# Moving four weight buffers by 64 to 384 bytes in on-chip memory

## The chip, the cores and the metric

The kernel runs on one core of a Trainium2 chip. The metric is the device time of one execution in microseconds (us), taken as the median of several runs. The profile comes from one further execution, recorded by the hardware profiler. The engines are named as in the profile: PE multiplies matrices, PEld is PE's loading of the stationary operand, DVE, ACT and POOL work elementwise, and SP issues most DMA transfers. A partition is one of the 128 rows of the on-chip memory; a "byte offset" below is always an offset within a partition, and "remainder" means the remainder of such an address divided by 2048.

## The reference, cut to what matters

One layer of a sequence model over 512 positions of width 1024, everything in float32. The large products are these:

```python
def _token_mixer(h, ...):
    p = h @ w_in                                    # 1024 -> 3 gates, pooling, latents, u and v
    ...
    y_a = _pool_mixer(a, w_pool, s_pool) @ w_branch[0]
    y_b = _mla(cq, ckv, kr, ...) @ w_branch[1]      # attention, 8 heads
    y_c = _sgu(uv, g_sg, b_sg, w_s, b_s) @ w_branch[2]
    merged = gates[:, :, 0] * y_a + gates[:, :, 1] * y_b + gates[:, :, 2] * y_c
    return merged @ w_o

def _conv_ffn(h, w_up, conv_w, conv_b, w_down):
    z = h @ w_up                                    # 1024 -> 2 * 2816
    ...                                             # causal convolution of width 3
    return (jax.nn.silu(gate) * val) @ w_down       # 2816 -> 1024

def reference(x, c, pos, ...):
    mod = silu(c) @ w_ada[l] + b_ada[l]             # six rows of 1024
    h = _modulate(x, sh_t, sc_t)
    y = _token_mixer(h, ...)
    x = _layer_norm(ALPHA * x + gt_t * y) * ln_t_g[l] + ln_t_b[l]
    h = _modulate(x, sh_f, sc_f)
    y = _conv_ffn(h, ...)
    x = _layer_norm(ALPHA * x + gt_f * y) * ln_f_g[l] + ln_f_b[l]
```

The positions' angles (`_rope_tables`) go through a reduction to one period before sine and cosine; two small tiles of the kernel, `ang` and `kq`, hold them.

## The kernel before

Every float32 operand is split into a high part and a low part in the type float32r: `hi = round(x)`, `lo = x - hi`. A product is then three matrix multiplications, high times low, low times high and high times high, added up in one PSUM tile.

The activations stay on chip. They lie in tiles of 128 partitions by 512 floats (2048 bytes a partition), with 48 buffers in the pool tag `act`, 16 in `h`, 8 in `m` and 8 in `pt`, all in the pool `sb`. The weights stream in. One chunk of weights is 128 by 1024 floats (512 KB): SP's queue loads it into one of three buffers `raw`, ACT casts it to the high part (`whi`, two buffers, line 91), and DVE subtracts to get the low part (`wlo`, two buffers, line 92). The function `wsplit` does this; `prepare`, `scaled_chunk` and `early_split` do the same for the first projection, for the two output projections (there POOL first scales the chunk) and for two chunks at the start of the second half. Both tags have two buffers that take turns, so one chunk is split while PE works on the one before.

PE uses a chunk 24 times, mostly in one of two forms. In `mm_chunk` (lines 112, 113 and 115) the stationary operand is a slice of 128 columns of the chunk and the moving operand is an activation tile of 512 columns: 16 multiplications with the high part (each slice twice, with the low and the high activations), then 8 with the low part. In `uv_half` (lines 846, 848, 849) and in the first loop of `project_out` (lines 1043, 1045, 1046) the stationary operand is a slice of an activation tile and the moving operand is half a chunk: 16 with the high part, then 8 with the low part. For each multiplication PE has a load of its own stationary operand, and the load for the next one runs while the present one streams its moving columns.

A few multiplications read other tiles. The padded tiles (`pad_t`, 528 floats) hold the softmax numerators `pe`, the gated products `uz` and the split rows `adah` and `adal`. `ptp` (line 661) transposes `pe`, `ptz` (line 954) transposes `uz`, and `pgt` (line 744) multiplies `adah` and `adal` by the constant matrix `onesr`.

Where the tiles lie follows from the pools, which are laid out one behind the other: `const`, then `pd` (five padded tiles of 2112 bytes), `sb`, `wp` (the weight buffers) and `sm`. All tiles of `sb` and, before the change, of `wp` are 2048 or 4096 bytes long, so all of them have the same remainder of 2048: 896 in the built program. The padded tile number i (0 to 4) ends up 320 - 64 i bytes short of that remainder, since 2112 is 2048 + 64 and five of them lie ahead of `sb`. `onesr` lies 416 bytes short of it. [...]

The order of the instructions on each engine is set by a scheduler when the kernel is built, within the order of the program text; `issue_after` adds a few constraints.

Of the kernel before, what the change touches and what calls it, by code (L numbers as in the profile page):

```python
# [8 lines left out]
F32 = mybir.dt.float32  # L9
F32R = mybir.dt.float32r  # L10
# [5 lines left out]
P = 128  # L16
S = 512
D = 1024
KT = 8
TT = 4  # L20
# [30 lines left out]
def trunk(ctx: ExitStack, tc: tile.TileContext, A, out):  # L51
    nc = tc.nc

    const = ctx.enter_context(tc.tile_pool(name="const", bufs=1))
    pd = ctx.enter_context(tc.tile_pool(name="pd", bufs=5))
    sb = ctx.enter_context(tc.tile_pool(name="sb", bufs=1))
    wp = ctx.enter_context(tc.tile_pool(name="wp", bufs=2))
# [3 lines left out]
    def ps(name):  # L61
        return pp.tile([P, 512], F32, name=name, tag="ps")
# [4 lines left out]
    def h_t(name, dt=F32R):  # L67
        return sb.tile([P, 512], dt, name=name, tag="h", bufs=16)
# [4 lines left out]
    def pt_t(name, dt=F32):  # L73
        return sb.tile([P, 512], dt, name=name, tag="pt", bufs=8)

    def pad_t(name, dt=F32):
        return pd.tile([P, 528], dt, name=name, tag="pad")

    def f(ap):
        return ap.bitcast(F32)  # L80

    def load(src, n, name):
        raw = wp.tile([P, D], F32, name=name, tag="raw", bufs=3)
        nc.sync.dma_start(out=raw[:, :n], in_=src)
        return raw

    def wsplit(src, n, name):
        raw = load(src, n, name)
        hi = wp.tile([P, D], F32R, name=name + "h", tag="whi")
        lo = wp.tile([P, D], F32R, name=name + "l", tag="wlo")  # L90
        nc.scalar.copy(out=hi[:, :n], in_=raw[:, :n])  # L91
        ins = nc.vector.tensor_tensor(  # L92
            out=lo[:, :n], in0=raw[:, :n], in1=f(hi[:, :n]), op=ALU.subtract
        )
        last_lo[:] = [ins.ins]
        return hi, lo
# [94 lines left out]
    nc.vector.tensor_scalar_add(out=bmod[:, :, 1], in0=cols[:, C_SCT : C_SCT + 8], scalar1=1.0)  # L191


    ang = const.tile([P, TT, 32], F32, name="ang")
    kq = const.tile([P, TT, 32], F32, name="kq")
    cosT, sinT, cosQ, sinQ = (
        const.tile([P, TT, 32], F32, name=name) for name in ("cosT", "sinT", "cosQ", "sinQ")
    )
# [109 lines left out]
    def after_split():  # L308
        order = ExitStack()
        for ins in split_done:  # L310
            order.enter_context(tc.issue_after(ins))
        return order
# [11 lines left out]
    def chunk(key):  # L324
        if key not in plan:
            return wsplit(A[key[0]][key[1:]], D, key[0])
        i = used[0]
        assert plan[i] == key
        for j in (i, i + 1):
            if j < len(plan) and j not in split:  # L330
                split[j] = wsplit(A[plan[j][0]][plan[j][1:]], D, plan[j][0])
        used[0] += 1
        return split[i]
# [55 lines left out]
    def prepare(j):  # L389
        raws = first_raw[j]  # L390
        acc = first_acc[j]
        wh = wp.tile([P, D], F32R, name="w0h", tag="whi")
        wl = wp.tile([P, D], F32R, name="w0l", tag="wlo")
        with after_split():
            for raw, a, b in ((raws[0], 0, NL), (raws[1], NL, NS)):
                nc.scalar.copy(out=wh[:, a:b], in_=raw[:, : b - a])
                nc.gpsimd.tensor_tensor(
                    out=wl[:, a:b], in0=raw[:, : b - a], in1=f(wh[:, a:b]), op=ALU.subtract
                )
        w0s.append((wh, wl))  # L400
        pm = ps("pm")
        for i in range(2):
            for part in range(2):
                nc.tensor.matmul(
                    pm[:, i : i + 1], acc[part][:, i * P : (i + 1) * P], ones[:, 0:1],
                    start=part == 0, stop=part == 1,
                )
        md = sm.tile([P, 2], F32, name="md", tag="md")
        for i in range(2):
            nc.scalar.activation(  # L410
                md[:, i : i + 1], pm[:, i : i + 1], AF.Identity, bias=bmod[:, j, i : i + 1]
            )
        pt = ps("pt")
        for t in range(TT):
            nc.tensor.transpose(
                pt[:, t * P : (t + 1) * P], xs[t][j // 4][:, (j % 4) * P : (j % 4 + 1) * P], ident
            )
        full = pad_t("hfull")
        hh = h_t(f"hT{j}h")
        hl = h_t(f"hT{j}l")  # L420
        nc.scalar.activation(hh, pt, AF.Identity, bias=md[:, 0:1], scale=md[:, 1:2])
        hi = nc.scalar.activation(full[:, :512], pt, AF.Identity, bias=md[:, 0:1], scale=md[:, 1:2])
        lo = nc.gpsimd.tensor_tensor(out=hl, in0=full[:, :512], in1=f(hh), op=ALU.subtract)
        split_done[:] = [hi.ins, lo.ins]
        hT_hi.append(hh)
        hT_lo.append(hl)
# [97 lines left out]

    def rotary_queries():
        wh, wl = wsplit(A["wqr"], D, "wqr")
        for t in range(TT):
            pq = ps("pq")
# [287 lines left out]
    for g in range(4):  # L816
        if g % 2 == 0:
            wh, wl = chunk(("wpool", g // 2))
# [189 lines left out]
    def scaled_chunk(src, gt, name, dst=None):  # L1008
        raw = load(src, D, name)
        for n in range(2):  # L1010
            c = slice(n * 512, (n + 1) * 512)
            nc.gpsimd.tensor_tensor(out=raw[:, c], in0=raw[:, c], in1=gt[n], op=ALU.mult)  # L1012
        if dst is None:
            hi = wp.tile([P, D], F32R, name=name + "h", tag="whi")
            lo = wp.tile([P, D], F32R, name=name + "l", tag="wlo")
            nc.scalar.copy(out=hi, in_=raw)  # L1016
            nc.vector.tensor_tensor(out=lo, in0=raw, in1=f(hi), op=ALU.subtract)  # L1017
            return [hi[:, :512], hi[:, 512:]], [lo[:, :512], lo[:, 512:]]
        his = [dst(f"{name}h{n}") for n in range(2)]
        los = [dst(f"{name}l{n}") for n in range(2)]  # L1020
        for n in range(2):
            c = slice(n * 512, (n + 1) * 512)
            nc.scalar.copy(out=his[n], in_=raw[:, c])
            nc.vector.tensor_tensor(out=los[n], in0=raw[:, c], in1=f(his[n]), op=ALU.subtract)
        return his, los

    def project_out(src, nk, resident, left_hi, left_lo, gt, dst, chain, name):
        acc = [[ps("py" + name) for _ in range(2)] for _ in range(TT)]

        def step(t, n, k, w):  # L1030
            ts_ = slice(t * P, (t + 1) * P)
            mm3(acc[t][n], left_hi[k][:, ts_], left_lo[k][:, ts_], w[0][n], w[1][n], k == 0, k == nk - 1)

        for k in range(nk - resident):
            w = scaled_chunk(src(k), gt, name)
            for rest in range(2):
                for t in range(TT):
                    ts_ = slice(t * P, (t + 1) * P)
                    hh, hl = left_hi[k][:, ts_], left_lo[k][:, ts_]
                    for n in range(2):  # L1040
                        o = acc[t][n]
                        if rest:
                            nc.tensor.matmul(o, hh, w[1][n], start=False, stop=False)  # L1043
                        else:
                            nc.tensor.matmul(o, hh, w[0][n], start=k == 0, stop=False)  # L1045
                            nc.tensor.matmul(o, hl, w[0][n], start=False, stop=False)  # L1046
        ws = {k: scaled_chunk(src(k), gt, f"{name}{k}", dst) for k in range(nk - resident, nk)}
        for t in range(TT):
            for n in range(2):
                for k in range(nk - resident, nk):  # L1050
                    step(t, n, k, ws[k])
            chain(t, acc[t])
# [11 lines left out]
    def early_split(m):  # L1064
        raw = load(A["wup"][m], D, "wup")
        if m in (2, 3):
            wh = wp.tile([P, D], F32R, name="wuph", tag="whi")
            wl = wp.tile([P, D], F32R, name="wupl", tag="wlo")
            uh = [wh[:, :512], wh[:, 512:]]
            ul = [wl[:, :512], wl[:, 512:]]  # L1070
        else:
            alloc = pt_t if m < 2 else act_t
            uh = [alloc(f"uph{m}{n}", F32R) for n in range(2)]
            ul = [alloc(f"upl{m}{n}", F32R) for n in range(2)]
        for n in range(2):
            nc.scalar.copy(out=uh[n], in_=raw[:, n * 512 : (n + 1) * 512])
        early[m] = uh, ul, raw
# [90 lines left out]
    def after_mixer(t, py):  # L1168
        py_o[t] = py
        if t == 0:  # L1170
            early_split(0)
            early_low(0, nc.vector)
            residual_in(0)
            early_split(1)
            early_low(1, nc.gpsimd)
            residual_in(1)
            residual(0, 0)
            residual(0, 1)
            rs_o[0] = ln_finish(st_o[0])
            affine(0)  # L1180
            early_split(2)
            early_low(2, nc.vector)
# [69 lines left out]
    for i in range(NP):  # L1252
        half = []
        for v in range(2):
# [11 lines left out]
            t = pt_t("zc")  # L1266
# [162 lines left out]
```

## Time and profile before

| | |
|---|---|
| median of 2 runs | 991.12 us (990.82 to 991.42) |
| profiled execution | 992.78 us, of which 990.8 us from the first to the last instruction |
| mean granted PE clock | 0.989 of full speed |
| busy: PE, PEld, DVE, ACT, POOL | 956.8, 802.3, 593.8, 392.8, 310.0 us |
| instructions on PE | 4530 multiplications, 4530 loads of a stationary operand |
| read from HBM | 116.30 MB |

A busy time is the time in which the engine had at least one instruction under way. Multiplications overlap in PE's pipeline, so one of them is recorded as longer than the distance to the next. In groups, "389/389/391" are the shortest, the median and the longest duration in nanoseconds, and what follows is when the first and the last of them began.

### The profile page before, as it was taken

The page shows a single profiled execution, that of the slowest core. Times are in us where ns is not written, and L with a number is a line of the kernel's source. Part 1 is how long each engine was busy: PE and PEld are TensorE (multiplying, and loading weights), DVE is VectorE, ACT ScalarE, POOL GpSimd, SP SyncE. Part 2 cuts the span into 40 slices and gives each one's busy share as a digit, 9 for nine tenths or more (in the row PEclk, how much of TensorE's full clock was granted, in tenths as well). Part 3 has the DMA queues.
Part 4 walks back from the last instruction along what each step waited for, and adds up shares of the span by engine and source line. Part 5 has one row for each costly group of instructions (what it writes and reads, how often), then busy time and mean ns, then how long its engine had stood idle before and what let it go on. Part 6 is the DMA issues. An engine that isn't in the chain of part 4 may idle for free.

```text
span 990.8 us, 12225 instructions
## 1 busy us (share of the span) xinstructions
PE 956.8 (97%) x4530; PEld 802.3 (81%) x4530; DVE 593.8 (60%) x923; ACT 392.8 (40%) x656; POOL 310.0 (31%) x311
## 2 busy tenths in 40 slices
PE   4999999999999999999999997999999999999996
PEld 3888888888878888888888876998888888888885
DVE  6947666556686565555433577675655565632367
ACT  3565555543333322422323235554444444422121
POOL 3555111222350022200012756321111121666654
PEclk9999999999999999999999998999999999999999
DMA  9713112135434633373222371133334343343222
GB/s 341 270 36 99 41 59 55 55 101 176 140 126 164 207 118 107 101 246 111 64 96 96 101 249 76 43 112 124 118 116 126 108 136 98 107 127 102 90 85 85
DMA packets 45274, 119.18 MB, mean 120 GB/s; under 512 B 5280, under 2 KB 8736, under 8 KB 45216
## 3 DMA queue, kind: packets, MB, share of 16 engines
q1 hardware_dynamic: 44784, 118.25, 36.5%
q8 instruction: 35, 0.57, 0.2%
q10 hardware_dynamic: 432, 0.17, 0.1%
q14 instruction: 23, 0.19, 0.1%
HBM read 116.30 MB, written 2.10 MB: 119 GB/s over the span
## 4 chain that ended last, share of the span: by engine, by line
PE 82%; DVE 6%; DMA 4%; POOL 3%; issue 2%; ACT 1%; SPq 0%; DVEq 0%; POOLq 0%; ACTq 0%
PE pzu L113 7%; PE pzu L112 7%; PE pzu L115 7%; PE pg L112 4%; PE pg L115 4%; PE pg L113 4%; PE py L112 3%; PE py L113 3%; PE pyd L1045 3%; PE py L115 3%; PE pyd L1043 3%; PE pyd L1046 3%; PE pu L849 3%; PE pu L848 3%; PE pu L846 3%
## 5 line engine op out<-in xcount | busy, mean ns | idle before, releaser
L92 DVE TENSOR_TENSOR wupl<-wup,wuph 128x1024 fp32r<-128x1024 f32 x38 | 47.8, 1258 | 71.8 <-PE pzu L115 45.8
L1012 POOL TENSOR_TENSOR d<-d,gtfb 128x512 f32<-128x512 f32 x44 | 74.3, 1710 | 37.6 <-DMA d<-in_wdn 34.8
L1285 POOL TENSOR_TENSOR zc<-zc 128x512 f32<-128x512 f32 x22 | 29.7, 1349 | 173.7 <-ACT zc L1284 154.1
L379 POOL TENSOR_TENSOR mg<-mg,th 128x512 f32<-128x512 f32 x16 | 31.3, 1958 | 144.1 <-DVE th L376 144.0
L1017 DVE TENSOR_TENSOR dl<-d,dh 128x1024 fp32r<-128x1024 f32 x18 | 29.1, 1614 | 56.2 <-PE pyd L1043 51.0
L91 ACT CAST wuph<-wup 128x1024 fp32r<-128x1024 f32 x38 | 39.9, 1050 | 46.5 <-PE pzu L113 46.5
L92 DVE TENSOR_TENSOR wgl<-wg,wgh 128x1024 fp32r<-128x1024 f32 x22 | 26.9, 1223 | 47.8 <-ACT wgh L91 35.1
L91 ACT CAST wbh<-wb 128x1024 fp32r<-128x1024 f32 x24 | 25.3, 1054 | 69.4 <-PE py L113 50.2
L726 DVE SCALAR_TENSOR_TENSOR ada<-adar,cact,ada 128x512 f32<-128x512 f32 x56 | 49.7, 918 | 0.5 <-DMA adar<-in_ada 0.5
L1016 ACT CAST dh<-d 128x1024 fp32r<-128x1024 f32 x18 | 19.0, 1053 | 62.5 <-PE pyd L1046 37.6
L1267 ACT ACTIVATE zc<-pzu,cols 128x512 f32<-128x512 f32 x44 | 34.2, 779 | 22.1 <-PE pzu L115 17.4
L91 ACT CAST wgh<-wg 128x1024 fp32r<-128x1024 f32 x22 | 23.3, 1059 | 40.1 <-PE pg L113 26.1
L92 DVE TENSOR_TENSOR wsgl<-wsg,wsgh 128x1024 fp32r<-128x1024 f32 x16 | 19.6, 1226 | 32.1 <-ACT wsgh L91 26.2
L92 DVE TENSOR_TENSOR wbl<-wb,wbh 128x1024 fp32r<-128x1024 f32 x24 | 31.0, 1290 | 9.7 <-ACT wbh L91 5.5
L91 ACT CAST wsgh<-wsg 128x1024 fp32r<-128x1024 f32 x16 | 16.8, 1053 | 48.7 <-PE pu L849 44.1
L1270 DVE SCALAR_TENSOR_TENSOR zc<-pzu,cols,zc 128x511 f32<-128x511 f32 x44 | 32.6, 744 | 3.9 <-ACT zc L1267 3.9
L647 POOL TENSOR_SCALAR pe<-pe,mx 128x128 f32<-128x128 f32 (+3 forms) x32 | 17.0, 534 | 54.3 <-DVE mx L646 53.9
L1274 DVE SCALAR_TENSOR_TENSOR zc<-pzu,cols,zc 128x510 f32<-128x510 f32 x44 | 32.6, 745 | 0.8
L1012 POOL TENSOR_TENSOR o<-o,gttb 128x512 f32<-128x512 f32 x16 | 26.7, 1693 | 16.9 <-DMA o<-in_wo 13.8
L1284 ACT ACTIVATE zc<-zc 128x512 f32<-128x512 f32 x22 | 13.9, 631 | 40.5 <-DVE zc L1274 40.4
L779 POOL TENSOR_TENSOR asum<-apad 128x527 f32<-128x527 f32 x8 | 12.2, 1520 | 55.4 <-ACT apad L774 29.3
L376 DVE SCALAR_TENSOR_TENSOR th<-th,py 128x512 f32<-128x512 f32 x16 | 11.0, 686 | 30.9 <-PE py L115 30.9
(1423 smaller groups left out, 3173.9 us busy)
## 6 DMA issues: line engine op xcount, KB each, us to landing
wup<-in_wup SPq DMA_DIRECT2D x44, 512.0 KB, 3.6
adar<-in_ada SPq DMA_DIRECT2D x64, 256.0 KB, 3.8
wb<-in_wb SPq DMA_DIRECT2D x24, 512.0 KB, 3.6
wg<-in_wg SPq DMA_DIRECT2D x22, 512.0 KB, 3.5
d<-in_wdn SPq DMA_DIRECT2D x22, 512.0 KB, 3.5
ada<-in_ada SPq DMA_DIRECT2D x32, 256.0 KB, 5.1
wsg<-in_wsg SPq DMA_DIRECT2D x16, 512.0 KB, 3.5
wa<-in_wa SPq DMA_DIRECT2D x8, 512.0 KB, 3.5
```

Of the source, the lines that this page charges most:

```text
L91: nc.scalar.copy(out=hi[:, :n], in_=raw[:, :n])
L92: ins = nc.vector.tensor_tensor(out=lo[:, :n], in0=raw[:, :n], in1=f(hi[:, :n]), op=ALU.subtract)
L112: nc.tensor.matmul(o, wh[:, c], xl[k], start=k == 0, stop=False)
L113: nc.tensor.matmul(o, wh[:, c], xh[k], start=False, stop=False)
L115: nc.tensor.matmul(o, wl[:, c], xh[k], start=False, stop=k == KT - 1)
L379: nc.gpsimd.tensor_tensor(out=merged[m], in0=merged[m], in1=th, op=ALU.add)
L726: nc.vector.scalar_tensor_tensor(out=acc[n], in0=src, scalar=cact[:, k : k + 1], in1=acc[n], op0=ALU.mult, op1=ALU.add,)
L846: nc.tensor.matmul(pu[t], hh, wl[:, c], start=False, stop=k == KT - 1)
L1012: nc.gpsimd.tensor_tensor(out=raw[:, c], in0=raw[:, c], in1=gt[n], op=ALU.mult)
L1267: nc.scalar.activation(t, pz, AF.Identity, bias=cols[:, cc + 3 : cc + 4], scale=cols[:, cc + 2 : cc + 3])
L1270: nc.vector.scalar_tensor_tensor(out=t[:, 1:512], in0=pz[:, 0:511], scalar=cols[:, cc + 1 : cc + 2], in1=t[:, 1:512], op0=ALU.mult, op1=AL ...
L1274: nc.vector.scalar_tensor_tensor(out=t[:, 2:512], in0=pz[:, 0:510], scalar=cols[:, cc : cc + 1], in1=t[:, 2:512], op0=ALU.mult, op1=ALU.add,)
```

## The change

The four weight buffers get a tag and a length each. A buffer is made longer by 16 floats (`whi`) or 32 floats (`wlo`), and the program uses it from behind that gap on. The pool lays the four out in the order `whi0`, `wlo0`, `whi1`, `wlo1`. Each gap pushes the buffer itself and all later ones along, so the used parts begin 64, 192, 256 and 384 bytes past the common remainder. The three `raw` buffers behind them move by 384 bytes too. The buffers still take turns by a counter. To make room, `ang` and `kq` (512 bytes each) leave the pool `const` and become the first two tiles of the rotating tag `pt`; this shifts the whole of `pd`, `sb` and `wp` down by 1024 bytes, with no effect on the distances between `pd` and `sb`.

With line numbers left aside, the built programs have the same instructions on every engine, in the same order and with waits on the same semaphores.

```diff
+    homes = {"whi": (16, 16), "wlo": (32, 32)}
+    turns = {"whi": 0, "wlo": 0}
+
+    def w_t(name, tag):
+        i = turns[tag] % 2
+        turns[tag] += 1
+        skip = homes[tag][i]
+        t = wp.tile([P, D + skip], F32R, name=name, tag=f"{tag}{i}", bufs=1)
+        return t[:, skip:]
+
...
     def wsplit(src, n, name):
         raw = load(src, n, name)
-        hi = wp.tile([P, D], F32R, name=name + "h", tag="whi")
-        lo = wp.tile([P, D], F32R, name=name + "l", tag="wlo")
+        hi = w_t(name + "h", "whi")
+        lo = w_t(name + "l", "wlo")
...
-    ang = const.tile([P, TT, 32], F32, name="ang")
-    kq = const.tile([P, TT, 32], F32, name="kq")
+    ang, kq = (
+        pt_t(name)[:, :128].rearrange("p (t f) -> p t f", f=32) for name in ("ang", "kq")
+    )
```

The same two lines are replaced in `prepare`, `scaled_chunk` and `early_split`.

More of the change, by code (lines that the diff above doesn't have):

```diff
@@ L391, in prepare @@
         acc = first_acc[j]
-        wh = wp.tile([P, D], F32R, name="w0h", tag="whi")
-        wl = wp.tile([P, D], F32R, name="w0l", tag="wlo")
+        wh = w_t("w0h", "whi")
+        wl = w_t("w0l", "wlo")
         with after_split():
@@ L1013, in scaled_chunk @@
         if dst is None:
-            hi = wp.tile([P, D], F32R, name=name + "h", tag="whi")
-            lo = wp.tile([P, D], F32R, name=name + "l", tag="wlo")
+            hi = w_t(name + "h", "whi")
+            lo = w_t(name + "l", "wlo")
             nc.scalar.copy(out=hi, in_=raw)
@@ L1066, in early_split @@
         if m in (2, 3):
-            wh = wp.tile([P, D], F32R, name="wuph", tag="whi")
-            wl = wp.tile([P, D], F32R, name="wupl", tag="wlo")
+            wh = w_t("wuph", "whi")
+            wl = w_t("wupl", "wlo")
             uh = [wh[:, :512], wh[:, 512:]]
```

## The prediction, made before the changed kernel had run

> **What bounds the kernel now.** I read the chain of waits first, to see which engine sets the end, then the chain piece by piece in the long stage of the up-projection, then PE's instructions one by one.
>
> ```profile
> PE 82%; DVE 6%; DMA 4%; POOL 3%; issue 2%; ACT 1%; SPq 0%; DVEq 0%; POOLq 0%; ACTq 0%
> 658.58 1.81 PE pzu L115 x8
> 664.01 1.81 PE pzu L115 x8
> 669.46 1.81 PE pzu L115 x8
> ```
>
> 82% of the span is PE following itself. In the stage shown the eight multiplications with the low part of a chunk come round every 5.44 us (669.46 - 658.58 is 10.88 for two chunks), which is 24 multiplications at 226.7 ns. Nothing is waited for there: whatever changes the distance between two multiplications changes the end by the same amount. The timeline of PE shows what that distance is made of.
>
> ```profile
> 652.00 0.28 PE L106 MATMUL pzu<-h2T4h,upl 128*128 128x256 f32 x1
> ...
> 654.64 0.28 PE L107 MATMUL pzu<-h2T7h,uph 128*128 128x256 f32 x1
> 654.76 0.40 PE L112 MATMUL pzu<-h2T0l,wuph 128*128 128x512 f32 x1
> ...
> 655.92 0.39 PE L113 MATMUL pzu<-h2T2h,wuph 128*128 128x512 f32 x1
> ...
> 660.23 0.39 PE L112 MATMUL pzu<-h2T0l,wuph 128*128 128x512 f32 x1
> ```
>
> Columns are start, duration, instruction. From 652.00 to 654.64 lie 22 distances between multiplications of 256 columns: 120.0 ns each. At 512 columns it is 226.7 ns. So 256 more columns cost 106.7 ns, 512 would cost 213.3, and 13.3 ns per multiplication are left that do not grow with the columns. The rhythm is not there at once either: the first five distances after 654.76 take 1.16 us, 27 ns more than five regular ones (1.133); the 19 from 655.92 to 660.23 take 4.31, which is regular. A disturbed PE needs some multiplications to fall into step.
>
> **What the change does to these.** No instruction is added, removed or moved. The only thing that can have a price is where the operands lie. Today the stationary operand that is loaded while a multiplication streams and the operand that it streams differ by a multiple of 512 bytes almost everywhere. After the change the weights lie 64, 192, 256 or 384 bytes off. Does PE care? The trace has a few multiplications with such offsets. The clearest are the gates' last ones between two heads of the attention, ahead of a transpose that loads a padded tile.
>
> ```profile
> L115 PE MATMUL pg<-hT7h,wgl x7: 391/393/400, 110.8 to 197.4; 128*128 128x512 f32 x7
> L113 PE MATMUL pg<-hT7h,wgh x7: 389/389/389, 109.0 to 194.0; 128*128 128x512 f32 x7
> L115 PE MATMUL pg<-hT7h,wgl 128*128 128x512 f32 x1 | 0.4, 393 | 0.0
> L115 PE MATMUL pg<-hT7h,wgl 128*128 128x512 f32 x1 | 0.4, 400 | 0.0
> ...
> L115 PE MATMUL pg<-hT7h,wgl 128*128 128x512 f32 x1 | 0.4, 391 | 0.0
> ```
>
> Both groups stream the same tile `hT7h`. Before another gate slice comes next (line 113) it is always 389 ns; before a padded tile it is 391 to 400. The single rows are from windows around each of the seven; in order of time they are 393, 400, 400, 391, 393, 393, 400; by the built program the padded tile lies 256, 64, 320, 128, 192, 256 and 64 bytes short of the streamed one's remainder. Equal offsets give equal times (256: 393 twice; 64: 400 twice). I take from this that the offset matters, by 2 to 11 ns, although the loaded tile is also of another type (f32) and the 389 ns have no f32 load behind them, so a part may be the type's. No value is below 389.
>
> The second place has float32r on both sides: four multiplications of line 744 among the up-projection, with offsets that are no multiples of 512 (the streamed padded tiles, and `onesr` 416 bytes short).
>
> ```profile
> 806.88 0.39 PE L115 MATMUL pzu<-h2T7h,wupl 128*128 128x512 f32 x1
> ...
> 808.04 0.39 PE L112 MATMUL pzu<-h2T0l,wuph 128*128 128x512 f32 x1
> ...
> 809.66 0.39 PE L113 MATMUL pzu<-h2T3h,wuph 128*128 128x512 f32 x1
> L744 PE MATMUL pgt<-adah,onesr 128*128 128x512 f32 x2 | 0.8, 398 | 0.0
> L744 PE MATMUL pgt<-adal,onesr 128*128 128x512 f32 x2 | 0.8, 394 | 0.0
> L113 PE MATMUL pzu<-h2T1h,wuph 128*128 128x512 f32 x1 | 0.4, 397 | 0.0
> L113 PE MATMUL pzu<-h2T2h,wuph 128*128 128x512 f32 x1 | 0.4, 395 | 0.0
> L113 PE MATMUL pzu<-h2T0h,wuph 128*128 128x512 f32 x1 | 0.4, 393 | 0.0
> L112 PE MATMUL pzu<-h2T1l,wuph 128*128 128x512 f32 x1 | 0.4, 393 | 0.0
> L112 PE MATMUL pzu<-h2T3l,wuph 128*128 128x512 f32 x1 | 0.4, 393 | 0.0
> L112 PE MATMUL pzu<-h2T0l,wuph 128*128 128x512 f32 x1 | 0.4, 392 | 0.0
> L115 PE MATMUL pzu<-h2T7h,wupl 128*128 128x512 f32 x1 | 0.4, 391 | 0.0
> L112 PE MATMUL pzu<-h2T2l,wuph 128*128 128x512 f32 x1 | 0.4, 389 | 0.0
> ```
>
> The 12 distances from 806.88 to 809.66 take 2.78 us, 60 ns more than 12 regular ones (2.72). The 12 durations exceed 389 by 2 x 9 + 2 x 5 + 8 + 6 + 4 + 4 + 4 + 3 + 2 + 0 = 59 ns. So an excess in duration is an excess in distance. And back among aligned operands, from 808.04 on, seven distances take 1.62 us, 33 ns too many, before the rhythm is back: leaving step costs more than the odd multiplications themselves.
>
> Third, the first projection's gates stream `hT` against slices that lie 256 bytes to either side of the aligned place.
>
> ```profile
> L105 PE MATMUL g0ps<-hT7l,w0h x2: 389/390/392, 66.7 to 67.4; 128*128 128x512 f32 x2
> L107 PE MATMUL g0ps<-hT7h,w0h x2: 389/391/393, 67.2 to 67.8; 128*128 128x512 f32 x2
> ```
>
> The minima, 389, are those of the second slice: with an offset of 256 PE falls into step and stays. So step does not need offset 0; one constant offset can do.
>
> **The sum.** How many multiplications read a moved buffer is counted by the subtractions that fill it, 24 per chunk.
>
> ```profile
> L92 DVE TENSOR_TENSOR wupl<-wup,wuph x38: 1211/1226/1929, 651.6 to 851.8; 128x1024 fp32r<-128x1024 f32 x38
> L92 DVE TENSOR_TENSOR wbl<-wb,wbh x24: 1215/1220/1889, 211.2 to 550.7; 128x1024 fp32r<-128x1024 f32 x24
> L92 DVE TENSOR_TENSOR wgl<-wg,wgh x22: 1202/1226/1227, 65.6 to 527.7; 128x1024 fp32r<-128x1024 f32 x22
> L92 DVE TENSOR_TENSOR wsgl<-wsg,wsgh x16: 1218/1226/1227, 304.4 to 452.8; 128x1024 fp32r<-128x1024 f32 x16
> L92 DVE TENSOR_TENSOR wal<-wa,wah x8: 1215/1224/1227, 184.1 to 273.2; 128x1024 fp32r<-128x1024 f32 x8
> L92 DVE TENSOR_TENSOR wpooll<-wpool,wpoolh x2: 1539/1668/1798, 290.1 to 295.7; 128x1024 fp32r<-128x1024 f32 x2
> L1017 DVE TENSOR_TENSOR dl<-d,dh x18: 1224/1522/2346, 857.3 to 949.8; 128x1024 fp32r<-128x1024 f32 x18
> L1017 DVE TENSOR_TENSOR ol<-o,oh x2: 1844/1902/1961, 556.9 to 563.0; 128x1024 fp32r<-128x1024 f32 x2
> ```
>
> That is 38 + 24 + 22 + 16 + 8 + 2 + 18 + 2 = 130 chunks, 3120 multiplications (some 250 smaller uses left out), 707 us at 226.7 ns. Within a chunk the offset is constant for 16 multiplications (high part) and then for 8 (low part), so it changes twice per chunk, 260 times. Bounds for one multiplication: from -13.3 ns (the fixed part gone) to +11 ns (400 against 389).
>
> What I take: a change of offset throws PE out of step, and it falls in again, as it did after 654.76 and 808.04, at 27 to 33 ns. 260 x 27 = 7.0 us, 260 x 33 = 8.6 us. The lower end of this term is 0, if a change of offset alone does not break step; I take 7 because the one multiplication at 806.88, in step until then, was at 391 as soon as an odd offset followed.
>
> The rest costs nothing. DVE's subtraction today has both inputs and its output at one remainder, and its median is 1220 to 1226 ns in every group that POOL leaves alone; if spreading them made it faster, DVE would only wait longer for PE. `ang` and `kq` do the same work in another place:
>
> ```profile
> L229 ACT ACTIVATE cosT<-kq x1: 309/309/309, 57.0 to 57.0; 128x128 f32<-128x128 f32 x1
> L545 POOL TENSOR_TENSOR qro<-qtA,qtB x4: 740/846/1187, 87.1 to 92.8; 128x256 f32<-128x256 f32 x4
> ```
>
> The last reading of `kq` ends at 57.3. As the first two of eight buffers of `pt` they come round again behind four `cn`, `qtA` and `qtB`, with the first `qro` at 87.1: 30 us of cover; without it POOL would wait by what is missing.
>
> The profiled execution took 992.78 us, 1.66 above the median of 991.12; I put the term on the median: 991.1 + 7.0 = 998.
>
> **The rivals.**
>
> *No effect at all, 991 us.* For it: groups with offset 256 reach 389. Against it: 391 to 400 above. [...]
>
> *PE stays out of step at odd offsets.* Then each multiplication has the mean excess of the unsettled ones: from 4 ns (the five of lines 112 and 113 from 808.04 to 808.97: 392, 393, 393, 397, 389, mean 3.8) to 6.7 ns (the seven gates, mean 395.7). 3120 x 4 = 12.5, 3120 x 6.7 = 20.9: 1004 to 1012 us.
>
> *The other side, clearly slower.* The offset of 64 bytes is the one that showed 400. If offsets of 64 and 192 hold PE at +11 ns in all buffers' turns, 3120 x 11 = 34 us: 1025. From a mean of 6.4 ns on (19.8 us over 3120) it is over 2%. Against it: 128 and 192 short showed 391 and 393.
>
> *Faster: the fixed 13.3 ns come from loading and streaming at the same remainder, and go.* 3120 x 13.3 = 41.6 us: 950; if it works for two of the four buffers, half of it: 970. For it: offsets of 64, 192 or 384 bytes occur in this trace for single multiplications only, so no steady stretch shows what the 13.3 ns do there. Against it: no duration under 389 at any odd offset. [...] The trace has 226.7 in every steady stretch.
>
> **How the numbers follow.** Falls in again: 0.35, 998 us. No effect: 0.22. Stays out of step: 0.17, of which 0.05 past 2%. Clearly slower: 0.07. Faster: 0.19, of which 0.16 past 2%. About 2% (971 to 1011) is what a measurement of this kernel can tell from no change. So faster 0.16, same 0.72, slower 0.12. The range leaves out the 1025 of the slower rival (0.07) and the larger gains (0.12): from 968, just past half the gain, to 1012, the end of staying out of step.
>
> **What would show it.** Falling in again: line 115's groups go from 389/389/389 to a higher maximum in the first multiplications of a part (`h2T0h,wupl`), and keep 389 in the last ones; 5.44 us per chunk become about 5.50. No effect: 389 throughout. Staying out: medians of 393 to 396 in all groups of lines 112 to 115. Faster: 24 multiplications take under 5.3 us. My working is wrong if the distance in a steady stretch of one offset is anything but 226.7 ns, or if the change of time lies outside the stages that read weight buffers.

## The result and the profile after

The changed kernel takes 1003.59 us (median of 2 runs, 1003.27 to 1003.91) against 991.12 us. The ratio is 1.0126, with a 95% interval from 1.0082 to 1.0169: 1.3% slower, within the 2% that counted as no change, and inside the predicted range. The profiled execution has a span of 1002.0 us against 990.8 and a granted clock of 0.991 against 0.989.

The chain of waits and its pieces in the up-projection, after the change:

```profile
PE 83%; POOL 5%; DVE 4%; issue 3%; DMA 3%; ACT 1%; SPq 0%; DVEq 0%; POOLq 0%; ACTq 0%
680.55 1.86 PE pzu L125 x8
686.07 1.86 PE pzu L125 x8
691.66 1.86 PE pzu L125 x8
697.17 1.86 PE pzu L125 x8
```

PE still follows itself. The eight multiplications with the low part (line 115 has become 125) now take 1.86 us instead of 1.81, and they come round after 5.52 and 5.59 us by turns (686.07 - 680.55, 691.66 - 686.07) instead of 5.44: the two pairs of buffers have different prices. Two neighbouring chunks show where in them the time goes. The timeline of PE, start and duration in us:

```profile
700.27 0.39 PE L122 MATMUL pzu<-h2T3l,wuph 128*128 128x512 f32 x1
...
702.37 0.40 PE L123 MATMUL pzu<-h2T7h,wuph 128*128 128x512 f32 x1
...
704.69 0.39 PE L123 MATMUL pzu<-h2T0h,wuph 128*128 128x512 f32 x1
...
705.84 0.39 PE L122 MATMUL pzu<-h2T3l,wuph 128*128 128x512 f32 x1
...
707.88 0.40 PE L123 MATMUL pzu<-h2T7h,wuph 128*128 128x512 f32 x1
708.12 0.41 PE L125 MATMUL pzu<-h2T0h,wupl 128*128 128x512 f32 x1
...
709.98 0.39 PE L122 MATMUL pzu<-h2T0l,wuph 128*128 128x512 f32 x1
```

- Offset 64, from 700.27 to 702.37: 9 distances in 2.10 us, 233.3 ns each, in the middle of a long part. This is a steady rhythm of its own, not a disturbance that dies out.
- Offset 256, from 704.69 to 705.84: 5 distances in 1.15 us, 230 ns; then from 705.84 to 707.88 nine in 2.04 us, 226.7 ns. Here PE falls in again. DVE runs the same two lines beside this stretch (1281 from 705.86, 1285 from 706.64) and beside the one at offset 64 (from 700.27 and 701.53), so its work is an unlikely cause of the difference.
- Offset 384, from 708.12 to 709.98: 8 distances in 1.86 us, 232.5 ns.

The groups of line 125 say the same in durations, which were 389/389/389. The medians of the eight groups are now 394 to 400; two of the longer ones:

```profile
L125 PE MATMUL pzu<-h2T0h,wupl x38: 397/400/405, 663.7 to 870.2; 128*128 128x512 f32 x38
L125 PE MATMUL pzu<-h2T6h,wupl x38: 396/397/398, 665.1 to 871.6; 128*128 128x512 f32 x38
```

By stage the loss follows the weight chunks. The first gate stands 1.3 us earlier than before; from then on the same pieces of the chain come later: 2.0 us later at the first `pmc` and 4.0 us at the second one. Before and after:

```profile
71.85 1.81 PE pg L115 x8
351.62 1.68 PE pmc L753 x16
465.91 1.68 PE pmc L753 x16
860.82 1.81 PE pzu L115 x8
958.74 1.81 PE pyd L1043 x8
```

```profile
70.58 1.85 PE pg L125 x8
353.60 1.68 PE pmc L764 x16
469.88 1.68 PE pmc L764 x16
870.32 1.86 PE pzu L125 x8
958.79 1.86 PE pyd L1054 x8
969.85 1.86 PE pyd L1054 x8
```

At the end of the up-projection it is 9.5 us, at the end of the streamed part of the output projection 11.1, and 11.2 over the whole span.

### The profile page after: what moved, and what is told of

Its sections match the earlier page's. It is cut to its first block, busy times and chain, and to the rows that moved or that the text cites. A ratio compares the mean times of both kernels' runs of the same rounds, so it can differ in the third digit from the quotient of the medians.

```text
span 1002.0 us, 12225 instructions
## 1 busy us (share of the span) xinstructions
PE 967.0 (97%) x4530; PEld 801.2 (80%) x4530; DVE 592.8 (59%) x923; ACT 392.9 (39%) x656; POOL 315.3 (31%) x311
## 4 chain that ended last, share of the span: by engine, by line
PE 83%; POOL 5%; DVE 4%; issue 3%; DMA 3%; ACT 1%; SPq 0%; DVEq 0%; POOLq 0%; ACTq 0%
PE pzu L125 7%; PE pzu L123 7%; PE pzu L122 7%; PE pg L125 4%; PE pg L122 4%; PE pg L123 4%; PE py L125 4%; PE py L123 3%; PE py L122 3%; PE pyd L1054 3%; PE pyd L1057 3%; PE pyd L1056 3%; PE pu L857 3%; PE pu L860 3%; PE pu L859 3%
## 5 line engine op out<-in xcount | busy, mean ns | idle before, releaser
L1023 POOL TENSOR_TENSOR o<-o,gttb 128x512 f32<-128x512 f32 x16 | 27.2, 1720 | 16.5 <-DMA o<-in_wo 15.1
```

## The experiments

The theory with which the experiments were chosen: what sets the distance between two multiplications is the offset, modulo 256 bytes, between the operand being streamed and the one being loaded meanwhile. Its rivals: the moved tiles `ang` and `kq` (or the shift of everything behind them), the change of offset rather than the offset, and the address itself.

### The move without the gaps

```diff
-    homes = {"whi": (16, 16), "wlo": (32, 32)}
+    homes = {"whi": (0, 0), "wlo": (0, 0)}
```

> The tiles ang and kq are moved as in the change (so everything behind them lies 1024 bytes lower), but the four weight buffers get no gap: all lie at the common remainder again. Theory 'offset' (the distance between two multiplications is set by the offset between the operand that is loaded and the one that is streamed): 226.7 ns everywhere, 991 us. Rival 'move' (the moved tiles, or the shift of everything by 1024 bytes, cost the time): about 1003 us.

Measured: 993.10 us against 991.97 for the kernel before, run beside it, ratio 1.0013 (1.0003 to 1.0022). The 1.3% are not in the move. The remaining 0.13% is not explained by it either, since the kernels with all four buffers at 256 bytes and with the low parts 256 bytes off, below, contain the same move and show none.

### All four buffers 256 bytes along

```diff
+    homes = {"whi": (64, 0), "wlo": (0, 0)}
```

> As the changed kernel, but with one gap of 256 bytes ahead of the first weight buffer and none ahead of the others, so that all four lie 256 bytes past the common remainder. Theory 'offset' with a period of 256: steady distance 226.7 ns in both forms, 991 us. If the period is 512 or longer: another steady distance, and a time that differs by 3120 times the difference (at 233 ns, 1012 us).

Measured: 991.77 us, ratio 0.9998 (0.9989 to 1.0007). The chain in the up-projection is back at 5.44 us per chunk:

```profile
712.58 1.81 PE pzu L125 x8
718.02 1.81 PE pzu L125 x8
```

An offset of 256 bytes is as good as none: 5.44 us per chunk, as before.

### All four buffers 64 bytes along

```diff
+    homes = {"whi": (16, 0), "wlo": (0, 0)}
```

> One gap of 64 bytes ahead of the first weight buffer and none ahead of the others: all four lie 64 bytes past the common remainder, and the offset never changes within a stage. Theory 'offset sets a steady distance': lines 112 to 115's form stays at 233.3 ns through whole chunks, 94 chunks x 24 x 6.7 ns = 15.0 us, the form with weights streamed (36 chunks, about 229 ns) 2 us: 1008 us. Rival 'falling in again' (my forecast's likeliest case: only a change of offset costs, 27 to 33 ns): there are no changes within a stage, so 991 us.

Measured: 1007.67 us, ratio 1.0156 (1.0139 to 1.0173). The forecast's likeliest case expected 991 here, since no offset changes within a stage, and falls. The chain of this kernel, first in the up-projection (weights loaded, activations streamed), then in the output projection (the other way round):

```profile
723.16 1.87 PE pzu L125 x8
728.76 1.87 PE pzu L125 x8
...
897.29 1.83 PE pyd L1054 x8
902.79 1.83 PE pyd L1054 x8
```

5.60 us per chunk is 233.3 ns per multiplication through whole chunks; 5.50 us is 229 ns. It is tempting to read this as the sign: the loaded operand 64 bytes ahead of the streamed one costs 6.7 ns, 64 bytes behind it about 2.3. The chain of the same kernel does not bear that out. Another stage streams the weights too (`pu`, the two calls of `uv_half`), with the loaded operand 64 bytes behind both times:

```profile
314.93 1.86 PE pu L857 x8
320.53 1.87 PE pu L857 x8
...
428.65 1.83 PE pu L857 x8
434.15 1.83 PE pu L857 x8
```

The same lines of the program, at the same offset, take 5.60 us per chunk the first time and 5.50 the second. So one offset can hold two steady rhythms, and the runs do not show what picks one. Where the weights are loaded the durations alternate from one multiplication to the next, and repeat in every chunk:

```profile
L125 PE MATMUL pzu<-h2T2h,wupl x38: 393/393/393, 667.5 to 875.6; 128*128 128x512 f32 x38
L125 PE MATMUL pzu<-h2T3h,wupl x38: 398/398/398, 667.7 to 875.8; 128*128 128x512 f32 x38
```

The sum from these rows is 94 x 24 x 6.7 = 15.1 and 36 x 24 x 2.3 = 2.0, 17.1 us, and 17.9 with the eight chunks of the first pass of `pu` at 6.7; the medians differ by 15.7. Where the rest went was not followed up.

### High parts in place, low parts 256 bytes off

```diff
+    homes = {"whi": (0, 64), "wlo": (64, 64)}
```

> Gaps chosen so that both buffers of high parts lie at the common remainder (0 and 512 bytes past it) and both of low parts 256 bytes off (256 and 768). The offset changes twice a chunk, between two values at which PE keeps 226.7 ns. Rival 'falling in again': each of 260 changes costs 27 to 33 ns, so 998 to 1000 us. Theory 'offset' with a period of 256: the change costs nothing, 991 us.

Measured: 991.75 us, ratio 0.9998 (0.9988 to 1.0009).

```profile
710.81 1.81 PE pzu L125 x8
716.25 1.81 PE pzu L125 x8
```

5.44 us per chunk: a change between two offsets that are multiples of 256 costs nothing. The 27 to 33 ns of the prediction are what PE needs to fall in after a stretch out of step, not the price of a change as such.

### Everything 64 bytes along

```diff
+    const.tile([P, 16], F32, name="gap")
     kst = const.tile([P, N_CONST], F32, name="kst")
```

> The kernel before with 64 unused bytes ahead of everything: activations and weights both move by 64 bytes, so all absolute addresses change by 64 and no offset between them does. If the offset between two operands counts: 226.7 ns, 991 us. If the address itself counts: 233 ns as at 64 bytes in the changed kernel, about 1008 us.

Measured, in one run: 991.20 us beside 992.03 for the kernel before, and 5.44 us per chunk on average. Here and below, single runs are compared; 25 runs of the kernel before, taken beside the first four experiments, spread from 990.77 to 994.29 us, so differences of 12 us and more stand clear of that spread and those under 3 us do not.

```profile
711.47 1.81 PE pzu L115 x8
716.90 1.81 PE pzu L115 x8
722.35 1.81 PE pzu L115 x8
```

The same 64 bytes that cost 15.7 us between weights and activations cost nothing when both move. It is the offset between the two operands that counts, not the address.

### Two surveys of other offsets

```diff
+    homes = {"whi": (8, 16), "wlo": (16, 16)}     # first survey: 32 and 160, 96 and 224 bytes
+    homes = {"whi": (4, 8), "wlo": (8, 8)}        # second survey
```

> As the changed kernel with other gaps: the buffers of high parts lie 32 and 160 bytes past the common remainder, those of low parts 96 and 224. Four more offsets in one look, to be read from the distances in the up-projection; the sum follows from them. With a period of 256 and a smooth curve between 226.7 (0) and 233.3 (64): 32 near 230, 96 to 160 near 232, 224 near 230, so about 1003 us. If some offset lets PE go under 226.7 ns, one of these shows it.

> The same with high parts at 16 and 80 bytes, low parts at 48 and 112. If the offset works in steps of 64 bytes, 16 and 48 read as 0 or 64 do (226.7 or 233.3 ns); if it is smooth, 16 lies near 228 and 48 near 232. About 1000 to 1005 us.

In the second survey the pool put each tile at the next multiple of 32 bytes, so that the four parts in fact lie at 16 and 96 (high), 64 and 128 (low); 48, 80 and 112 were not tried. Measured in one run each: 1013.39 and 1006.19 us, beside 992.03. The chain of the first survey, 5.60 and 5.62 us per chunk, none of its four offsets clearly better than the others:

```profile
726.07 1.87 PE pzu L125 x8
731.67 1.87 PE pzu L125 x8
...
900.70 1.88 PE pyd L1054 x8
906.32 1.87 PE pyd L1054 x8
```

I had expected a smooth curve between 0 and 64 bytes, but 32 already costs as much as 64 (233 ns each in the table below). The second survey shows 16 and 96 bytes in two neighbouring chunks:

```profile
724.00 0.39 PE L123 MATMUL pzu<-h2T3h,wuph 128*128 128x512 f32 x1
...
725.81 0.39 PE L123 MATMUL pzu<-h2T7h,wuph 128*128 128x512 f32 x1
...
728.13 0.39 PE L123 MATMUL pzu<-h2T0h,wuph 128*128 128x512 f32 x1
...
729.77 0.39 PE L122 MATMUL pzu<-h2T4l,wuph 128*128 128x512 f32 x1
```

At 16 bytes 8 distances take 1.81 us (226.3, so the aligned 226.7 within the last digit); at 96 seven take 1.64 us (234.3). But 16 bytes are not free either. Later in the same stage, in the same buffer:

```profile
845.69 0.39 PE L122 MATMUL pzu<-h2T0l,wuph 128*128 128x512 f32 x1
...
849.19 0.39 PE L123 MATMUL pzu<-h2T7h,wuph 128*128 128x512 f32 x1
```

These 15 distances take 3.50 us, 233.3 ns each. All 14 chunks at this offset up to 814.66 us settle at 226.7, and all five from 823.06 us on stay at 233.3. Between them stand the four multiplications with the padded tiles (`pgt`, 816.76 to 817.46 us). So at this offset too PE can run in either of two rhythms. That `pgt` threw it from the one into the other was not tested.

### Offsets under 32 bytes

```diff
+    homes = {"whi": (1, 59), "wlo": (58, 61)}
```

> As the changed kernel with gaps such that the high parts lie 4 and 524 bytes past the common remainder and the low parts 264 and 788: modulo 256 these are 4, 12, 8 and 20. Theory 'same group of 32 bytes' (16 showed the aligned distance, 32 did not): where the weights are loaded, 226.7 ns at all four. Where they are streamed the offset is negative (-4 to -20) and reaches into the group before: between 226.7 and 233.3 ns. Together about 993 us. If the offset had to be 0 within a few bytes: 233.3 ns, about 1010 us.

Measured in one run: 1007.15 us beside 994.45. The theory of a group of 32 bytes falls. The chain:

```profile
721.42 1.86 PE pzu L125 x8
727.00 1.85 PE pzu L125 x8
732.52 1.87 PE pzu L125 x8
...
894.72 1.86 PE pyd L1054 x8
900.26 1.89 PE pyd L1054 x8
905.91 1.86 PE pyd L1054 x8
```

The chunks take 5.58 and 5.52 us where the weights are loaded, and 5.54 and 5.65 us where they are streamed, the longest of all. So offsets of 4, 8, 12 and 20 bytes cost time too, against 5.44 us per chunk in the kernel before. No run here shows the cause, and the price does not simply grow with the offset: 16 bytes show 233.3 ns as well as 226.7, and 32 and 64 cost as much as 20 (233 ns each).

All surveys together, from the starts of single multiplications in the up-projection (the last eight with the high part, or five in the second half of the low part, of one chunk; weights loaded, so the offset is counted from the streamed activation to the loaded weight, modulo 256; 8, 12 and 20 were laid at 264, 524 and 788):

| offset, bytes | 0 | 4 | 8 | 12 | 16 | 20 | 32 | 64 | 96 | 128 | 160 | 192 | 224 | 256 |
|---|---|---|---|---|---|---|---|---|---|---|---|---|---|---|
| distance, ns | 226.7 | 232 | 231 | 230 | 226.7 or 233 | 233 | 233 | 233 | 234 | 231-233 | 233 | 233 | 233 | 226.7 |

A figure stands for the chunk that was read, not for the offset as such. At 12 bytes one gate's chunk holds 226.7 ns (131.76 to 135.16 us, 15 distances) and another 233.3 (176.56 to 180.06 us). For 128 the 231 are from the changed kernel, where the weight lies 384 bytes off, and the 233 from the second survey, where it lies 128 off, so a period of 256 is shown for multiples of 256 only. Nothing lies below 226.7. So none of the layouts tried is faster than the kernel before, and none was sought further.

### Padded tiles at multiples of 256 bytes

```diff
-        return pd.tile([P, 528], dt, name=name, tag="pad")
+        return pd.tile([P, 576], dt, name=name, tag="pad")
```

with the gaps at zero as in the first experiment.

> The moved ang and kq without gaps, and padded tiles of 2304 instead of 2112 bytes, so that each of the five lies a multiple of 256 bytes from the activations' remainder. This tests what the prediction read from the gates' last multiplication ahead of the padded tile pe. Theory 'offset': the seven of it (391, 393 and 400 ns before) become equal, near 393, which is what offset 256 showed. If the type of the loaded tile or the place in the program made the difference, they stay between 391 and 400. The time is 991 us either way: only some tens of multiplications are touched.

Measured in one run: 992.05 us beside 994.45. The seven gates' last multiplications ahead of the padded tile `pe`, which were 391/393/400:

```profile
L125 PE MATMUL pg<-hT7h,wgl x7: 392/392/393, 110.5 to 197.1; 128*128 128x512 f32 x7
```

They are equal now. In the kernel of the first experiment, with the same move and the old padded tiles, they are still 391/393/400. So their spread was the offset; the 3 ns that stay over 389 go with something else, perhaps the type of the loaded tile, which was not varied.

## Why the prediction was right, and where it was not

The forecast was no measurable change at 998 us, in a range from 968 to 1012; measured were 1003.59. The case that came true is not the one I held likeliest (0.35) but the third, "PE stays out of step at odd offsets" (0.17), with 1004 to 1012 us, whose lower end the time just misses. That the time lies in the range is owed to this rival, which set the range's upper end, and not to the step behind the 998. Its sum came out partly by luck: its 4 ns were a mean over unsettled multiplications, while the measured 4.0 is a mean over offsets that cost from nothing (256) to 6.7 ns (64).

- *The bound.* Right: a change in the distance between multiplications went into the end almost whole. After the change two chunks take 11.11 us where the weights are loaded and 11.06 where they are streamed, against 10.88; that is 4.8 ns and 3.75 ns per multiplication, 94 x 24 x 4.8 = 10.8 and 36 x 24 x 3.75 = 3.2, together 14.0 us. The medians differ by 12.5, the profiled spans by 11.2. Part of the difference is that the changed kernel's first gate in the profile stands 1.3 us earlier (line 115 at 71.85 before, line 125 at 70.58 after), ahead of the long PE-bound stages.
- *The offset matters, by 2 to 11 ns, and nothing goes under 389.* Right, and the experiment on the padded tiles shows that this reading of the 391 to 400 ns was sound. The row held more than I read: 320 bytes short gave 400, as 64 did, which fits a period of 256. For the size it was no guide: 3 ns of its mean excess of 6.7 stay at neutral offsets (392 against 389), and that the steady rhythm at 64 bytes costs 6.7 ns too is a coincidence.
- *"A change of offset throws PE out of step, and it falls in again."* This step failed. It took what happens at offsets of 0 and 256 to hold at any constant offset. The first projection's gates, on which it stood, were at 256 bytes either way, which the second experiment shows to be as good as none; the row could not tell the two readings apart. At 64 bytes PE has a steady rhythm of 233.3 ns, which is the sign of being wrong that the prediction named: a steady stretch of one offset at anything but 226.7. The step's own count was wrong as well: the change between neutral offsets is free (5.44 us per chunk with the low parts 256 bytes off). Falling in itself is real: PE does it at 256 bytes in the changed kernel (five distances of 230 ns, then 226.7), and at 16 bytes in 14 chunks of the up-projection out of 19 (226.7 ns).
- *The rest costs nothing.* Right within what was measured: the kernels with the move and harmless offsets are at 0.9998 twice and at 1.0013 once.
- *The rivals.* "No effect at all" fell: 64 bytes between PE's own two operands cost a multiplication 6.7 ns where the weights are loaded. "Clearly slower" needed a mean of 6.4 ns; it was 4.0 (12.5 us over 3120), since one of the four offsets, 256, is neutral and 384 costs about 4 ns where the weights are loaded. The kernel with all four at 64 came to 1.56%, and the first survey, at 1013.39 against 992.03 in one run each, to about 2.2%. "Faster" fell: over a dozen offsets none was under 226.7 ns, so the 13.3 ns per multiplication are not the price of equal remainders. What they are stays open.

Why the offset counts was not settled. The runs show that it is relative, that in the long stretches multiples of 256 bytes come back to 226.7 ns, and that at some other offsets (16, 12, and 64 behind) more than one rhythm can hold. What picks the rhythm stays open. The runs show no counter of conflicts; the recorded loads of the stationary operand hardly get longer (in the up-projection medians of 188 ns before and 187 to 192 after the change; all 4530 together were under way for 802.3 us before and for 802.1 with all four buffers at 64 bytes), and what waits for what inside PE's reads cannot be seen in the profile.

## What to carry to other kernels

When PE follows itself, read the distance between its multiplications to the nanosecond in a steady stretch, and look for the few places with another layout: equal tiles at equal remainders hide what an offset would cost. In this kernel the stationary operand being loaded and the moving operand being streamed should differ by a multiple of 256 bytes (226.7 ns in the long stretches of every kernel that had it, 229 to 235 at the other offsets but for some chunks at 12 and 16 bytes); tiles of whole kilobytes do that by themselves, and a tile padded to an odd length shifts all that follow it in its pool. A few samples show that an effect exists, but not what it does when it holds for a whole stage; for that, look for a stretch in which it is constant, and check that the stretch differs in the quantity that matters. The second survey adds a warning for the measurement too: one settled chunk showed 16 bytes as free, and five others of the same stage did not, so read a rhythm in several places before calling it the price.

## What the runs showed of the hardware that was not expected

- A constant offset of 64 bytes between loaded and streamed operand gives float32r multiplications of 512 columns a steady distance of 233.3 ns instead of 226.7; with the loaded operand 64 bytes behind it is 229 ns in some stages and 233.3 in others.
- Multiples of 256 bytes cost nothing (226.7 ns; 991.77 and 991.75 us against 991.97); with weights loaded, the chunks read at 4, 8, 12, 20, 32 and 64 to 224 bytes cost 3 to 8 ns per multiplication (230 to 234 ns). At 16 bytes PE holds 226.7 ns or 233.3, and in the up-projection it went from the one to the other behind four multiplications with other offsets.
- The excess in an instruction's duration repeats to the nanosecond in all 38 chunks (393/393/393 and 398/398/398 by turns at 64 bytes).
